# Loads of stored input differences two pairs ahead in the down projections of an encoder trunk

## The chip, the cores and the metric

The kernel runs on one core of one Trainium2 chip. The metric is the device time of one execution in microseconds (us). The core has a tensor engine (TensorE, PE in the profile; PEld is its weight load), a vector engine (DVE), a scalar engine (ACT), GpSimd (POOL) and a sync engine (SP) that only issues transfers; 16 DMA engines carry them. Each engine works through its own instructions in order.

## The reference

A trunk of two layers over 256 tokens of width 2048, in fp32. Each layer has one attention sub-layer and one MLP; the change touches the MLP only.

```
D_MODEL = 2048; SEQ = 256; DEPTH = 2; D_FF = 4 * D_MODEL
for i in range(DEPTH):
    h = rms_norm(x, norm_attn[i])
    ...
    # layer 0: differential attention, layer 1: windowed grouped-query attention with a sink,
    # both with 4 cross-attention heads into 256 memory tokens
    x = x + heads @ w_out[i]
    h = rms_norm(x, norm_mlp[i])
    x = x + jnp.square(jax.nn.relu(h @ w_up[i])) @ w_down[i]
```

## The kernel before

**Products.** Every fp32 operand is split into a rounded part hi (a cast on ACT, L439) and a remainder lo (a subtraction on DVE, L440), and every product is three matmuls: hi by hi, hi by lo, lo by hi (`three`, L531 to L533). A *piece* (`piece`, L417; `fetch`, L370) is a weight block of 128 x 1024 that SP loads (raw) and that is split so; a *pair* is two pieces, 256 rows of the weight. A pair is normally eight products (24 matmuls of 128 x 512). In the out, up and down projections some pairs take a seven-product scheme instead (`seven`, L548; 21 matmuls): it needs sums of weight blocks (made beforehand for layer 1 and part of layer 0 by two POOL transfers, a copy and an add in DRAM, L291 and L295, tiles *madesum*) and differences of the input blocks (`differences`, L538). In the down projection, the seven-product pairs are those of `FAST` (L50): 2, 4, 6, ..., 28 and 29 of 32.

**The MLP** (`mlp`, L984). The up projection ends in `to_hidden`: a block of hidden values is transposed, put through relu and square (ACT, L1020 and L1021), and for the blocks of `AWAY` stored to DRAM by POOL (L1024, *hid*), to be read back by SP later. A task some pairs later, `keep`, forms the differences of a seven-product pair j (128 x 2 x 512, hi and lo, 512 KB) in a tile of the tag "h2" and stores them to DRAM by POOL (L1000, *kept*). The down projection then runs twice over the 32 pairs, for the left and the right half of its 2048 columns. A pair of its loop asks for its first piece, for the split of the next pair's hidden block (`h2_of`, which also takes an "h2" tile; AHEAD is 2 pieces), for its second piece and, if it is a seven-product pair, loads its stored differences back into a further "h2" tile (L1118, `h<-kept`); then come its products. The stores of pairs 28 and 29 fall into the first pairs of the down projection.

**What sets the order.** The program is written in the order of these calls; the scheduler of the framework then places each engine's instructions by its own estimate of when they can run, so that an instruction can stand earlier or later in its engine's queue than in the code. The tag "h2" is a ring of six SBUF slots (`quad`, L91): a tile can only be written when all readers of the tile that held its slot before are done, a store to DRAM among them. Difference tiles to be stored, reloaded differences and hidden splits share this ring. The loads L1118 and the stores L1000 and L1024 stand in one queue on POOL, as do L291 and L295: a transfer that waits for its slot or its data holds up those behind it.

Of the kernel before, what the change touches and what calls it, by code (L numbers as in the profile page):

```python
# [22 lines left out]
P = 128  # L23
# [47 lines left out]
def trunk(ctx: ExitStack, tc: tile.TileContext, xin, xtok, memin, memtok, posrel, gcol, rows,  # L71
          w_a, w_b, w_mem, w_out, w_up, w_down, out):
    nc = tc.nc
# [188 lines left out]
    sums = {}  # L262
# [721 lines left out]
    def mlp(layer, X2, last):  # L984
        hT = []
        kept = {}
        wide = big([P, 6, 4, S])
        slots.clear()
        slots.extend(wide[:, i] for i in range(5))
        hidden_in.clear()  # L990

        def hidden(j):
            return hT[j // 2].rearrange("p k s -> p (k s)")[:, (j % 2) * 512:(j % 2) * 512 + 512]

        def keep(j):

            t2 = quad("h2", (P, 2, 512))
            differences(t2, hidden(j))
            kept[j] = dp.tile([P, 2, 512], F32R, name=nm("kept"))
            nc.gpsimd.dma_start(kept[j], t2)  # L1000

        name = f"up{layer}"
        diffs = {}

        def own_add(own, u):
            for n in range(2):
                for t in range(2):
                    nc.vector.tensor_tensor(u[n][t], own[n][t], u[n][t], op=ALU.add)

        def to_hidden(q, n, u, i, tag):  # L1010
            c = 2 * q + n
            if i == 0:
                hT.append(wide[:, 5] if c == 15 else blk([P, 4, S], F32))
            pt = bank(tag)
            for oo in range(2):
                for t in range(2):
                    o = 2 * i + oo
                    nc.tensor.transpose(out=pt[:, oo * S + t * P:oo * S + (t + 1) * P], in_=u[n][t][:, o * P:(o + 1) * P], identity=ident)  # L1018
            j = 2 * c + i
            nc.scalar.activation(hidden(j), pt, AF.Relu)  # L1020
            nc.scalar.activation(hidden(j), hidden(j), AF.Square)  # L1021
            if c in AWAY:
                hidden_in[j] = dp.tile([P, 512], F32, name=nm("hid"))
                nc.gpsimd.dma_start(hidden_in[j], hidden(j))  # L1024
            if any(j in fast_pairs(f"down{layer}", h) for h in range(2)):
                Task([Light(lambda: keep(j), 0)], wait=KEEP_AFTER[2 * n + i])

        for q in range(8):
            tag, other = ("mm", "aux") if q % 2 == 0 else ("aux", "mm")
            own = [[bank(tag) for _ in range(2)] for _ in range(2)]  # L1030
            fast = UP_FAST[q]
            for j in range(8):
                if j == fast[0]:
                    side = [bank(other) for _ in range(4)]
                if q == 0 and j in DIFF_UP:
                    i = DIFF_UP[j]
                    diffs[i] = quad("h2" if i == 2 else "blk", (P, 2, 512))
                    pair_differences(X2.pairs[i], diffs[i])
                two = [piece(name, q, 2 * j + i) for i in range(2)]
                pair = X2.pairs[j]  # L1040

                def at(kk, t, part):
                    return pair[:, kk, part, t * P:(t + 1) * P]

                if j in fast:
                    seven(own, side, j == fast[0], j == fast[-1], two, sums.pop((name, q, j)), at, diffs[j])
                elif j < 7:
                    for kk in range(2):
                        for t in range(2):
                            for n in range(2):  # L1050
                                one_of_eight(own, n, t, 2 * j + kk, KT - 1, two, at)
                else:
                    for n in range(2):
                        for t in range(2):
                            for kk in range(2):
                                one_of_eight(own, n, t, 2 * j + kk, KT - 1, two, at)
                if j == fast[-1]:
                    u = side_sums(side)
                for _ in range(2):
                    tick(2)  # L1060
            own_add(own, u)
            if q == 0:
                mlp_stats()
            Task([lambda q=q, u=u, n=n, i=i, tag=tag: to_hidden(q, n, u, i, tag) for n in range(2) for i in range(2)], wait=1, gap=0)
        slots.append(blk([P, 4, S], F32))
        N2 = Halves()
        while making:
            making.popleft()[1]()

        def h2_of(j):  # L1070
            t2 = quad("h2", (P, 2, 512))
            split(t2[:, 0, :], t2[:, 1, :], hids.pop(j) if j in hidden_in else hidden(j))
            return lambda kk, t, part: t2[:, part, kk * S + t * P:kk * S + (t + 1) * P]

        for half_ in range(2):
            tag = "mm" if half_ == 0 else "aux"
            ps = [[bank(tag) for _ in range(2)] for _ in range(2)]
            chunks = (2 * half_, 2 * half_ + 1)
            fast = fast_pairs(f"down{layer}", half_)
            plain_last = max(j for j in range(fast[-1]) if j not in fast)  # L1080

            def add_to(n, t, src, i=0):
                at = chunks[n] * 512 + i
                d = xt[:, t, at:at + src.shape[1]]
                nc.vector.scalar_tensor_tensor(d, src, r2[:, t:t + 1], d, op0=ALU.mult, op1=ALU.add)
                return at, d

            def finish(n, t, src, i=0):
                at, d = add_to(n, t, src, i)
                if last:  # L1090
                    nc.sync.dma_start(out[:, t * D + at:t * D + at + src.shape[1]], d)

            def by_columns(n, t):

                for i in (0, 256):
                    part_ = bank("mm")[:, 0:256]
                    for j, two, at in held:
                        for kk in range(2):
                            three(part_, j == held[0][0] and kk == 0, j == held[-1][0] and kk == 1,
                                  lambda part: at(kk, t, part), two[(kk + n) % 2], slice(n * 512 + i, n * 512 + i + 256))  # L1100
                    finish(n, t, part_, i)

            held = []
            ats = deque([h2_of(0)])
            for j in range(32):
                if j == fast[0]:
                    side = [bank("aux" if half_ == 0 else "mm") for _ in range(4)]
                two = [piece(f"down{layer}", half_, 2 * j)]
                if j < 31:
                    ats.append(h2_of(j + 1))  # L1110
                two.append(piece(f"down{layer}", half_, 2 * j + 1))
                at = ats.popleft()
                if last and half_ == 1 and j >= 30:
                    held.append((j, two, at))
                    continue
                if j in fast:
                    t2 = quad("h2", (P, 2, 512))
                    nc.gpsimd.dma_start(t2, kept[j])  # L1118
                    seven(ps, side, j == fast[0], j == fast[-1], two, sums.pop((f"down{layer}", half_, j)), at, t2)
                else:  # L1120
                    for kk in range(2):
                        for t in range(2):
                            for n in range(2):
                                own_last = 2 * plain_last + 1 if last and half_ == 1 and n == t == 1 else 4 * KT - 1
                                one_of_eight(ps, n, t, 2 * j + kk, own_last, two, at)
                if j == fast[-1]:
                    shared(side, add_to)
                    if last and half_ == 1:
                        add_to(1, 1, ps[1][1])
                for _ in range(2):  # L1130
                    tick(2)
            for n in range(2):
                for t in range(2):
                    if held and n == t == 1:
                        by_columns(n, t)
                        continue
                    for j, two, at in held:
                        for kk in range(2):
                            one_of_eight(ps, n, t, 2 * j + kk, 4 * KT - 1, two, at)
                    finish(n, t, ps[n][t])  # L1140
                if not last:
                    chunk_sq(chunks[n])
                    to_features(chunks[n], N2, G_ATTN + KT, tag)
        slots.clear()
        return N2
# [153 lines left out]
```

## Time and profile before

| | |
|---|---|
| time, median of 3 runs | 2088.14 us (2087.17, 2088.18, 2088.14) |
| the profiled execution's own time | 2087.19 us |
| its span | 2085.4 us |
| granted tensor clock, mean | 0.998 of full speed |
| busy: PE, DVE, ACT, POOL | 2073.3, 1771.0, 1275.6, 182.8 us |
| DMA, mean rate | 270 GB/s, 563.63 MB |
| loads of differences (L1118) | 59, of 512 KB each, median 5.8 us from issue to landing |

The down projection of layer 0 runs from about 770 us of the span on, that of layer 1 from about 1752 us to the end. A busy time says how long an engine had something to do; since the PE's matmuls overlap, a group's mean duration (some 390 ns) is longer than the distance from one start to the next. A wait is the idle time of an engine in front of an instruction, put down to the event that came last.

### The profile page before, as it was taken

To read this page: it belongs to the slowest core of one execution; us is meant where nothing else is said; L and a number is where in the kernel's file an instruction comes from. 1 tells how busy PE (TensorE), PEld (TensorE's weight loads), DVE (VectorE), ACT (ScalarE), POOL (GpSimd) and SP (SyncE) were. 2 spreads that over 40 slices of the span, in tenths; PEclk is the share of its full clock that TensorE was granted. 3 is DMA by queue.
4 is the path that set the end of the run, shared out by engine and by line. 5 is a ranking of instruction groups with operands and counts; after the bars stand their busy time and mean duration, and the time that the engine had idled before them with its cause. 6 is when DMAs were issued, how large, how long until landed. Compare 5 with 4: busy or idle time off the path is not lost.

```text
span 2085.4 us, 28771 instructions
## 1 busy us (share of the span) xinstructions
PE 2073.3 (99%) x10011; PEld 1721.3 (83%) x10011; DVE 1771.0 (85%) x2545; ACT 1275.6 (61%) x1892; POOL 182.8 (9%) x286
## 2 busy tenths in 40 slices
PE   9999999999999999999999999999999999999999
PEld 7878888888888878888888888888888887888887
DVE  7667778898999998899886677889999998889888
ACT  7457665566655666667655566566655666666664
POOL 1310100000011100000001100000001111000000
PEclk9999999999999999999999999999999999999999
DMA  9899864578899889988979975568889999998895
GB/s 315 300 295 280 264 206 157 189 255 245 266 288 300 257 289 314 338 279 294 330 267 287 266 233 198 170 210 242 252 273 300 285 282 346 306 332 305 295 332 170
DMA packets 168001, 563.63 MB, mean 270 GB/s; under 512 B 19456, under 2 KB 20480, under 8 KB 166656
## 3 DMA queue, kind: packets, MB, share of 16 engines
q1 hardware_dynamic: 132544, 439.62, 60.9%
q0 software_dynamic: 35168, 122.18, 21.9%
q8 instruction: 78, 1.28, 0.2%
q14 instruction: 67, 0.55, 0.1%
q10 hardware_dynamic: 144, 0.01, 0.0%
HBM read 531.19 MB, written 92.41 MB: 299 GB/s over the span
## 4 chain that ended last, share of the span: by engine, by line
PE 95%; DMA 2%; DVE 1%; issue 1%; ACT 1%; POOL 0%; SPq 0%; ACTq 0%; DVEq 0%; POOLq 0%
PE mm L531 12%; PE mm L532 12%; PE mm L533 12%; PE aux L532 11%; PE aux L533 11%; PE aux L531 11%; PE mm L492 7%; PE mm L493 7%; PE mm L494 7%; DMA h<-kept 1%; PE mm L1018 1%; PE aux L635 1%; DVE lo L440 1%; PE aux L612 1%; PE aux L654 1%
## 5 line engine op out<-in xcount | busy, mean ns | idle before, releaser
L439 ACT CAST hi<-raw 128x1024 fp32r<-128x1024 f32 (+1 forms) x522 | 525.4, 1036 | 451.1 <-issue 143.4
L440 DVE TENSOR_TENSOR lo<-raw,hi 128x1024 fp32r<-128x1024 f32 (+1 forms) x522 | 617.4, 1207 | 196.1 <-ACT hi L439 194.1
L492 PE MATMUL mm<-hi,x 128*128 128x512 f32 x640 | 256.0, 402 | 0.2 <-ACT hi L439 0.2
L493 PE MATMUL mm<-lo,x 128*128 128x512 f32 x640 | 251.0, 392 | 0.2 <-DVE lo L440 0.2
L494 PE MATMUL mm<-hi,x 128*128 128x512 f32 x640 | 250.3, 391 | 0.2 <-DVE x L436 0.2
L439 ACT CAST h<-big 128x1024 fp32r<-128x1024 f32 (+1 forms) x100 | 101.7, 1020 | 151.6 <-DVE big L283 129.6
L531 PE MATMUL mm<-hi,h 128*128 128x512 f32 (+1 forms) x461 | 179.8, 390 | 5.2 <-DMA h<-kept 5.0
L532 PE MATMUL mm<-lo,h 128*128 128x512 f32 (+1 forms) x461 | 179.1, 389 | 0.8 <-DVE lo L440 0.8
L533 PE MATMUL mm<-hi,h 128*128 128x512 f32 (+1 forms) x461 | 178.9, 388 | 0.0
L532 PE MATMUL aux<-lo,h 128*128 128x512 f32 x442 | 172.1, 389 | 0.1
L531 PE MATMUL aux<-hi,h 128*128 128x512 f32 x442 | 172.1, 390 | 0.0
L533 PE MATMUL aux<-hi,h 128*128 128x512 f32 x442 | 172.0, 389 | 0.0
L531 PE MATMUL mm<-hi,x 128*128 128x512 f32 x414 | 161.8, 391 | 0.0
L533 PE MATMUL mm<-hi,x 128*128 128x512 f32 x414 | 161.1, 389 | 0.0
L532 PE MATMUL mm<-lo,x 128*128 128x512 f32 x414 | 161.1, 389 | 0.0
L531 PE MATMUL aux<-hi,x 128*128 128x512 f32 x398 | 155.5, 391 | 0.0
L532 PE MATMUL aux<-lo,x 128*128 128x512 f32 x398 | 154.9, 389 | 0.0
L533 PE MATMUL aux<-hi,x 128*128 128x512 f32 x398 | 154.6, 389 | 0.0
L440 DVE TENSOR_TENSOR lo<-big,hi 128x1024 fp32r<-128x1024 f32 (+1 forms) x141 | 144.4, 1044 | 0.2 <-ACT hi L439 0.2
L494 PEld LDWEIGHTS mm<-hi,x 128*128 128x128 f32 x640 | 120.2, 188 | 26.1 <-DVE x L436 0.5
L492 PEld LDWEIGHTS mm<-hi,x 128*128 128x128 f32 x640 | 120.3, 188 | 24.7 <-ACT hi L439 1.0
L493 PEld LDWEIGHTS mm<-lo,x 128*128 128x128 f32 x640 | 120.5, 188 | 23.7 <-DVE lo L440 1.8
(309 smaller groups left out, 4193.7 us busy)
## 6 DMA issues: line engine op xcount, KB each, us to landing
raw<-in_w_up SPq DMA_DIRECT2D x164, 512.0 KB, 6.2
raw<-in_w_down SPq DMA_DIRECT2D x138, 512.0 KB, 5.7
madesum<-in_w_down POOLq DMA_DIRECT2D x118, 512.0 KB, 6.5
big<-in_w_up SPq DMA_DIRECT2D x92, 512.0 KB, 4.4
raw<-in_w_a SPq DMA_DIRECT2D x72, 512.0 KB, 5.5
h<-kept POOLq DMA_DIRECT2D x59, 512.0 KB, 5.8
raw<-in_w_out SPq DMA_DIRECT2D x52, 512.0 KB, 4.1
big<-madesum SPq DMA_DIRECT2D x49, 512.0 KB, 4.6
```

What stands on the lines that cost most here:

```text
L439: nc.scalar.copy(hi, src)
L440: return nc.vector.tensor_tensor(lo, src, as32(hi), op=ALU.subtract)
L492: nc.tensor.matmul(ps[t], lhsT=xh, rhs=hi[:, ws], start=(k == 0), stop=False)
L493: nc.tensor.matmul(ps[t], lhsT=xh, rhs=lo[:, ws], start=False, stop=False)
L494: nc.tensor.matmul(ps[t], lhsT=xl, rhs=hi[:, ws], start=False, stop=(k == KT - 1))
L531: nc.tensor.matmul(acc_, lhsT=x(0), rhs=w2[0][:, ws], start=first_, stop=False)
L532: nc.tensor.matmul(acc_, lhsT=x(0), rhs=w2[1][:, ws], start=False, stop=False)
L533: nc.tensor.matmul(acc_, lhsT=x(1), rhs=w2[0][:, ws], start=False, stop=last_)
L612: nc.tensor.transpose(out=pt[:, h * P:(h + 1) * P], in_=qn[t][:, h * P:(h + 1) * P], identity=ident)
L635: nc.tensor.transpose(out=pt[:, kt * S + qt * P:kt * S + (qt + 1) * P], in_=p_of(qt)[:, kt * P:(kt + 1) * P], identity=ident)
L654: nc.tensor.matmul(ps[c][:, qt * S:(qt + 1) * S], lhsT=qT[a][r, hl, qs], rhs=kT[b][r, hl, :], start=(a + b == 0), stop=(a == 1))
L1018: nc.tensor.transpose(out=pt[:, oo * S + t * P:oo * S + (t + 1) * P], in_=u[n][t][:, o * P:(o + 1) * P], identity=ident)
```

## The change

The load of a seven-product pair's differences is taken out of the pair's own place and put into a helper, `load_kept`, that takes the "h2" tile and issues the transfer. Pair j now calls it for pair j + 2, between its two pieces; a call ahead of the loop is for pair 1, which is not in `FAST` and so loads nothing. The first load of each half is that of pair 2, asked for by pair 0. Nothing is added to or taken from the computation.

```diff
             held = []
+            diff_in = {}
+
+            def load_kept(j):
+                if j in fast:
+                    diff_in[j] = quad("h2", (P, 2, 512))
+                    nc.gpsimd.dma_start(diff_in[j], kept[j])
+
+            load_kept(1)
             ats = deque([h2_of(0)])
             for j in range(32):
...
                 two = [piece(f"down{layer}", half_, 2 * j)]
                 if j < 31:
                     ats.append(h2_of(j + 1))
+                load_kept(j + 2)
                 two.append(piece(f"down{layer}", half_, 2 * j + 1))
...
                 if j in fast:
-                    t2 = quad("h2", (P, 2, 512))
-                    nc.gpsimd.dma_start(t2, kept[j])
-                    seven(ps, side, j == fast[0], j == fast[-1], two, sums.pop((f"down{layer}", half_, j)), at, t2)
+                    seven(ps, side, j == fast[0], j == fast[-1], two, sums.pop((f"down{layer}", half_, j)), at, diff_in.pop(j))
```

In the changed code the load is line 1109. The rows below are the engines' queues; the number behind a name is that of the tile, and it differs between the two kernels for the same tile.

**Layer 0, first pairs of the down projection, POOL.** L1000 stores differences (7629 those of pair 26, 7897 of pair 28, 7948 of pair 29), L1024 stores hidden blocks, L1118 loads the differences of pairs 2, 4 and 6 (kept_5310, 5565, 5692). Before:

```order
L1000 DMA kept_7629<-h_7622 128x1024
L1024 DMA hid_7816<-blk_7808 128x512
L1024 DMA hid_7825<-blk_7808 128x512
L1118 DMA h_7918<-kept_5310 128x1024
L1000 DMA kept_7897<-h_7890 128x1024
L1000 DMA kept_7948<-h_7941 128x1024
L1118 DMA h_8014<-kept_5565 128x1024
L1118 DMA h_8101<-kept_5692 128x1024
```

After:

```order
L1000 DMA kept_7629<-h_7622 128x1024
L1109 DMA h_7778<-kept_5310 128x1024
L1024 DMA hid_7818<-blk_7810 128x512
L1024 DMA hid_7827<-blk_7810 128x512
L1109 DMA h_7914<-kept_5565 128x1024
L1000 DMA kept_7899<-h_7892 128x1024
L1000 DMA kept_7950<-h_7943 128x1024
L1109 DMA h_8010<-kept_5692 128x1024
```

Each of the three loads has moved up: the first past two stores of hidden blocks, the second past the stores of pairs 28 and 29 into the place where the first load stood.

**The same place, PE.** These are products of pair 2; h_7859 (before) and h_7861 (after) are its hidden split, h_7918 and h_7778 its differences, and h_7909 is the hidden split of pair 3. Before:

```order
L531 MATMUL mm_7762<-hi_7862,h_7859 128x512
L532 MATMUL mm_7762<-lo_7863,h_7859 128x512
L533 MATMUL mm_7762<-hi_7862,h_7859 128x512
L531 MATMUL mm_7763<-x_7851,h_7859 128x512
L532 MATMUL mm_7763<-x_7852,h_7859 128x512
L533 MATMUL mm_7763<-x_7851,h_7859 128x512
L531 MATMUL mm_7762<-hi_7904,h_7909 128x512
L532 MATMUL mm_7762<-lo_7905,h_7909 128x512
L533 MATMUL mm_7762<-hi_7904,h_7909 128x512
L531 MATMUL mm_7764<-hi_7845,h_7918 128x512
```

After:

```order
L531 MATMUL mm_7762<-hi_7864,h_7861 128x512
L532 MATMUL mm_7762<-lo_7865,h_7861 128x512
L533 MATMUL mm_7762<-hi_7864,h_7861 128x512
L531 MATMUL mm_7764<-hi_7847,h_7778 128x512
L532 MATMUL mm_7764<-lo_7848,h_7778 128x512
L533 MATMUL mm_7764<-hi_7847,h_7778 128x512
L531 MATMUL aux_7902<-x_7851,h_7778 128x512
L532 MATMUL aux_7902<-x_7852,h_7778 128x512
L533 MATMUL aux_7902<-x_7851,h_7778 128x512
L531 MATMUL aux_7904<-x_7851,h_7778 128x512
```

Before, the seventh product of pair 2 and the first of pair 3 were placed ahead of the four that need the differences; now these four stand where the code has them. The same holds in layer 1; elsewhere PE's order is the same but for one product at the change of halves of layer 0.

**Layer 1, first pairs of the down projection, POOL.** L291 and L295 are the copies and adds of the weight sums; kept_14308, 14563 and 14690 are the differences of pairs 2, 4 and 6; the stores L1000 are those of pairs 28 and 29. Before:

```order
L291 DMA madesum_16737<-in_w_down 16x8192
L291 DMA madesum_16769<-in_w_down 16x8192
L295 DMA madesum_16737<-in_w_down 256x1x512
L295 DMA madesum_16769<-in_w_down 256x1x512
L1024 DMA hid_16826<-blk_16818 128x512
L1024 DMA hid_16835<-blk_16818 128x512
L1118 DMA h_16928<-kept_14308 128x1024
L1000 DMA kept_16907<-h_16900 128x1024
L1000 DMA kept_16958<-h_16951 128x1024
L1118 DMA h_17024<-kept_14563 128x1024
```

After:

```order
L291 DMA madesum_16737<-in_w_down 16x8192
L291 DMA madesum_16769<-in_w_down 16x8192
L1109 DMA h_16788<-kept_14308 128x1024
L295 DMA madesum_16737<-in_w_down 256x1x512
L295 DMA madesum_16769<-in_w_down 256x1x512
L1024 DMA hid_16828<-blk_16820 128x512
L1024 DMA hid_16837<-blk_16820 128x512
L1109 DMA h_16924<-kept_14563 128x1024
L1000 DMA kept_16909<-h_16902 128x1024
L1000 DMA kept_16960<-h_16953 128x1024
L1109 DMA h_17020<-kept_14690 128x1024
```

The first load now stands ahead of the two adds and two hidden stores, the second ahead of the stores of pairs 28 and 29.

**The same place, ACT, with the events that each cast waits for.** h_16978 and h_17015 (after: 16980 and 17017) are the hidden splits of pairs 4 and 5, h_17065 and h_17102 (17067 and 17104) those of pairs 6 and 7; hi_16981 (16983) belongs to pair 4's second piece, hi_17010 and hi_17019 (17012 and 17023) to pair 5. DMAHW stands for a landing of an SP transfer, DMASW for one of a POOL transfer; in the second list DMASW5 is the store of pair 28 and DMASW6 that of pair 29. Before:

```order
L439 CAST hi_16964<-big_13666 128x1024 [waits DMAHW6_49,DVE_49,PE_49]
L439 CAST h_16978<-blk_14481 128x512
L439 CAST hi_16981<-t2k_16853 128x512 [waits DMAHW5_49,PE_49]
L439 CAST h_17015<-blk_14481 128x512
L439 CAST h_17065<-blk_14496 128x512 [waits DMASW3_49,PE_49]
L439 CAST x_16970<-big_13666 128x1024 [waits DVE_49]
L439 CAST h_17102<-blk_14496 128x512 [waits DMASW5_49,Activation_49]
L439 CAST x_17055<-big_13666 128x1024 [waits DMAHW1_49]
L439 CAST hi_17010<-raw_17009 128x1024 [waits DMAHW6_49,PE_49]
```

After:

```order
L439 CAST hi_16966<-big_13666 128x1024 [waits DMAHW6_49,DVE_49,PE_49]
L439 CAST hi_16983<-t2k_16855 128x512 [waits DMAHW5_49,PE_49]
L439 CAST h_16980<-blk_14481 128x512 [waits DMASW5_49,DVE_49]
L439 CAST h_17017<-blk_14481 128x512 [waits DMASW7_49,PE_49]
L439 CAST x_16972<-big_13666 128x1024 [waits DVE_49]
L439 CAST h_17067<-blk_14496 128x512 [waits DMASW6_49,Activation_49]
L439 CAST x_17057<-big_13666 128x1024 [waits DMAHW1_49]
L439 CAST hi_17012<-raw_17011 128x1024 [waits DMAHW6_49,PE_49]
L439 CAST hi_17023<-raw_17022 128x1024 [waits DMAHW7_49,PE_49]
```

The hidden split of pair 4 (h_16980) waited for no transfer and now takes the slot of the differences of pair 28, so it waits for their store, with the cast of x behind it; that of pair 6 waits for the store of pair 29. In layer 0 the slots change hands in the same way.

## The prediction

> **What bounds the kernel now.** I read the page's busy times first, then what the tensor engine waited for, then a table by stages, and only then single instructions. In the rows of waits stand the us waited, how often, and the longest; in those of the stages (from:to, length) the busy us (and instructions) of PE, its weight loads, DVE, ACT and POOL, then the granted clock, the DMA engines' busy share and GB/s.
>
> ```profile
> PE 2073.3 (99%) x10011; PEld 1721.3 (83%) x10011; DVE 1771.0 (85%) x2545; ACT 1275.6 (61%) x1892; POOL 182.8 (9%) x286
> ...
> PE mm L531 <- DMA h<-kept: 5.0, 2, 2.6
> ...
> PE mm L532 <- DVE lo L440: 0.8, 1, 0.8
> ...
> 764.00:800.00 36.00, 33.38 (x154) 27.12 (x153) 30.59 (x41) 25.00 (x36) 3.78 (x8) 1.00 0.94 328
> 800.00:934.00 134.00, 134.00 (x593) 110.96 (x592) 119.78 (x139) 87.18 (x109) 6.87 (x13) 1.00 0.90 308
> ...
> 1750.00:1790.00 40.00, 36.67 (x157) 29.45 (x156) 31.17 (x42) 27.69 (x39) 4.37 (x8) 0.91 0.99 339
> ```
>
> PE is busy for 99% of the span, so nothing is won except where PE stands still or runs at a lower clock. Of 59 loads of differences (h<-kept, L1118) PE waited for two, 5.0 us in all. The table by stages says where: from 800 to 934 us PE has no idle time at all (134.00 of 134.00 us, 593 matmuls, so 0.226 us from one to the next), while the first 36 to 40 us of each layer's down projection lose 2.6 and 3.3 us, the second at a granted clock of 0.91. The ceiling of this change is therefore in two places: the first pairs of the down projection in layer 0 (from 770 us) and in layer 1 (from 1752 us). Everywhere else the other loads land in time already, and asking for them earlier can give nothing.
>
> **Layer 0, what goes.** PE's timeline, start and duration in us, in brackets the idle time before an instruction and what ended it:
>
> ```profile
> 775.66 0.39 PE L531 MATMUL aux<-hi,h 128*128 128x512 f32 x1
> ...
> 778.16 0.39 PE L533 MATMUL mm<-hi,h 128*128 128x512 f32 x1
> 781.03 0.51 PE L531 MATMUL mm<-hi,h 128*128 128x512 f32 x1 [2.48 <-DMA h<-kept]
> ...
> 790.35 0.50 PE L531 MATMUL mm<-hi,h 128*128 128x512 f32 x1
> ...
> 794.79 0.39 PE L532 MATMUL mm<-lo,h 128*128 128x512 f32 x1
> ```
>
> Pair 2, the first seven-product pair, starts at 775.66. From there to the second lo of pair 5 (794.79) are 21 + 24 + 21 + 4 = 70 matmuls, 15.8 us at 0.226; it took 19.13. So 3.3 us are lost, nearly all in front of the first load's product at 781.03, and 0.3 at the second's (790.35). Both loads stood late in POOL's queue:
>
> ```profile
> 771.76 1.08 POOL L1024 DMA_DIRECT2D hid<-blk  x2 [24.21 <-ACT blk L1021]
> 772.84 0.56 POOL L1118 DMA_DIRECT2D h<-kept  x1
> ...
> 755.76 0.39 PE L532 MATMUL mm<-h,blk 128*128 128x512 f32 x1
> ...
> 765.00:770.00 5.00, 5.00 (x31) 4.32 (x31) 5.00 (x7) 2.02 (x3) 0.00 (x0) 1.00 0.67 213
> ```
>
> The first load followed two stores of hidden blocks that waited 24 us for ACT. In the changed order it stands ahead of them and needs only its slot, whose last reader is the matmul at 755.76. It goes at about 756.3 and, even at the slowest landing seen (8.2 us, below), lands by 765, 12 us before pair 2 needs it. The DMA engines have room there (0.67 busy from 765 to 770). The second load takes the place of the first at 772.8 and lands by 781; pair 4 then starts at 785.9. Both waits go.
>
> **Layer 0, what is late next.** The loads now hold slots two pairs longer, so the ring of six "h2" slots hands out others. The hidden split of pair 4 gets the slot of the difference tile stored at 776.13 and that of pair 6 the one stored at 779.79, and both must wait for these stores to land; before, only one later split did.
>
> ```profile
> 786.89 0.62 ACT L439 CAST h<-blk 128x512 fp32r<-128x512 f32 x1 [1.19 <-DMA kept<-h]
> ...
> 789.45 2.36 DVE L440 TENSOR_TENSOR lo<-raw,hi 128x1024 fp32r<-128x1024 f32 x2
> ```
>
> That later split is visible: ACT goes on at 786.89, when the second store has landed. Behind it on ACT stand a cast of x and pair 5's two hi, and on DVE pair 5's two lo, ready at 789.45 + 2.36 = 791.81. PE, no longer held up, wants the second lo at 775.66 + 15.8 = 791.5. So the store takes over as the last wait, for 0.3 us, and the matmul of 794.79 comes at 791.9: **2.9 us saved** of 3.3. If the store lands 1 us later it is 1.9; if earlier, 3.3.
>
> **Layer 1, what goes.**
>
> ```profile
> 1757.88 0.39 PE L531 MATMUL aux<-hi,h 128*128 128x512 f32 x1
> ...
> 1761.28 0.50 PE L532 MATMUL mm<-lo,h 128*128 128x512 f32 x1 [0.76 <-DVE lo L440]
> ...
> 1764.58 0.79 PE L531 MATMUL mm<-hi,h 128*128 128x512 f32 x1 [2.57 <-DMA h<-kept]
> ...
> 1769.44 0.63 PE L533 MATMUL aux<-x,h 128*128 128x512 f32 x1
> ...
> 1775.66 0.39 PE L532 MATMUL mm<-lo,h 128*128 128x512 f32 x1
> ...
> 1765.00:1770.00 5.00, 5.00 (x13) 3.84 (x13) 2.04 (x3) 1.14 (x2) 0.53 (x1) 0.50 1.07 403
> ```
>
> From pair 2's start to the second lo of pair 4 (1775.66) are 21 + 24 + 4 = 49 matmuls, 11.1 us; it took 17.78. The 6.7 us are the wait for a lo of pair 3 that had been pulled ahead of the load's products (0.8), the wait for the load itself (2.6), and a halved clock: the granted clock is 0.50 from 1765 to 1770 and twelve matmuls (1764.58 to 1769.44 and its successor) run at 0.43 instead of 0.226 us, another 2.5. The changed PE order puts the load's products first again, so that lo has time.
>
> [...]
>
> **Layer 1, what is late next.** POOL, ACT and DVE, and the DMA share:
>
> ```profile
> 1737.70 1.02 POOL L291 DMA_DIRECT2D madesum<-in_w_down  x2 [7.93 <-DVE lo L440]
> ...
> 1759.60 0.54 POOL L1000 DMA_DIRECT2D kept<-h  x1 [2.65 <-DVE h L440]
> ...
> 1767.57 0.53 POOL L1118 DMA_DIRECT2D h<-kept  x1 [3.78 <-DMA kept<-h]
> ...
> 1766.79 0.61 ACT L439 CAST h<-blk 128x512 fp32r<-128x512 f32 x1
> ...
> 1770.63 1.04 ACT L439 CAST x<-big 128x1024 fp32r<-128x1024 f32 x1
> ...
> 1771.71 1.23 DVE L440 TENSOR_TENSOR x<-big,x 128x1024 fp32r<-128x1024 f32 x1 [4.67 <-ACT x L439]
> 1772.85 0.68 DVE L440 TENSOR_TENSOR lo<-t2k,hi 128x512 fp32r<-128x512 f32 x1
> ...
> 1740.00:1745.00 5.00, 5.00 (x23) 4.13 (x22) 5.00 (x9) 0.51 (x2) 1.09 (x1) 1.00 0.95 389
> ```
>
> The load now follows the two copies of 1737.70, at about 1738.8, long enough ahead. But the hidden split of pair 4 must now wait for the store issued at 1759.60. When that landed shows in POOL's row at 1767.57: about 1767.3. Behind this cast on ACT stand another h cast and the cast of x, behind that on DVE x and the second lo of pair 4: 1767.3 + 0.61 + 0.61 + 1.04 + 1.23 + 0.68 = 1771.5, against 1775.66 now. So at an unchanged landing **4.2 us** are saved of 6.7, and PE waits about 2.5 us in two parts instead.
>
> The landing won't stay unchanged. 512 KB that were asked for at 1756 now enter at 1738.8, and the second load stands where the first stood, ahead of the store. At 389 GB/s 0.52 MB are 1.35 us; the DMA engines were 0.95 busy then (and over 1.0 afterwards), which leaves a few tenths free. I take **1.0 us later**; the ends are 0, if the room suffices, and 2.8, if the load's own queue gets half of that rate. 4.2 - 1.0 = **3.2 us** in layer 1.
>
> POOL's queue already holds two copies there. [...]
>
> **What costs nothing.** No instruction is added: 59 loads before and after. Loads moved ahead of the stores of hidden blocks and of the madesum adds delay data that is read again only late in the down projection. In the steady stretch the hidden splits turn on four slots instead of six, and every second one stands behind two hi casts (about 2 us on ACT); the first row below says that they waited for PE, not PE for them, and PE had no idle time there. At the half change of layer 0 DVE makes a lo two operations earlier, PE wants it three matmuls earlier: 0 (ends -0.2 and +0.7).
>
> ```profile
> ACT h L439 <- PE aux L533: 32.3, 28, 2.7
> ...
> h<-kept POOLq DMA_DIRECT2D x59, 512.0 KB, 5.8
> ...
> L1118 POOL DMA_DIRECT2D h<-kept x59: 527/527/558, 772.8 to 2056.3; - x59
> ...
> DMA to landing us min/median/max: 3.7/5.8/8.2
> ```
>
> **Sum.** 2.9 + 3.2 = 6.1 us off the profiled execution's 2087.19 us (span 2085.4): 2081.1. The median of the runs shown is 2088.14, 0.95 above that execution; off the median it is 2082.0.
>
> **Rivals.**
> 1. *All stalls go* (the stores land 2 to 3 us sooner, as loads do at their fastest, 3.7 us): 3.3 + 6.7 = 10.0, so 2078.1. Against it: the DMA engines are full around both stores. Chance 0.13.
> 2. *The full queue takes layer 1's gain back*: the store lands 2.8 us later, and the t2k load that DVE waits for ahead of pair 2 comes 1.4 later too and puts the store itself off; nothing is left of 4.2, and 2.9 remain: 2085.2. For it: shares of 0.95 and more. Chance 0.17; a third of it stays above 4.2 us.
> 3. *The clock drops again*: the two waits that remain in layer 1 are within some 4 us, like the two that went ahead of 0.50. 6.1 - 2.5 = 3.6: 2084.5. For it the likeness, against it that they are shorter and layer 0's single wait cost no clock. Chance 0.10.
> 4. *It doesn't ask earlier*: POOL works its queue in order, and a load that is blocked by its slot would wait as before. 2088.1. The slots' last readers (755.76 in layer 0) speak against it. Chance 0.03.
> 5. *Slower*: in the steady stretch the hidden splits, now with four slots, reach PE too late. Each of the 57 remaining seven-product pairs would have to lose 0.18 us (10.3 us, the 6.1 gained and 4.2 more) before the kernel is slower by 0.2%; at 0.25 us each it is 2090. It decides once the splits slip by more than the three pairs (about 15 us) between slot and use; PE's 134.00 of 134.00 us speak against it. Chance 0.07.
>
> **The numbers.** Forecast 0.50, with a range of its own of 2080 to 2084. A measurement here can tell about 0.2% (4.2 us) from no change. Faster: 0.50 + 0.13 + 0.05 of rival 2 = 0.68. Within 0.2%: the rest of rival 2, rivals 3 and 4 = 0.25. Slower: 0.07. The range runs from rival 1 (2078.1) to rival 2 (2085.2), with about the 1.0 us on the slow side by which the runs shown differ: 2078 to 2086.5.
>
> **What would show it.** PE's waits for h<-kept vanish; ACT's "h <- DMA kept<-h" grows to several us around 783, 787, 1768 and 1771; the first loads go at about 756 and 1739; the clock is 1.00 from 1765 to 1770; the second lo of pair 5 in layer 0 comes at 791.9, that of pair 4 in layer 1 at 1775.66 - 3.2 - 2.9 = 1769.6. I am wrong if PE waits for the stores for more than 3 us in a layer, or loses time between 800 and 934.

## The result, and the profile after

| | before | after |
|---|---|---|
| median | 2087.65 us (10 runs) | 2083.26 us (10 runs) |
| lowest and highest | 2084.64 to 2089.64 | 2081.78 to 2085.18 |
| profiled execution, its span | 2087.19, 2085.4 | 2082.35, 2080.6 |

The ratio is 0.9981, 95% interval [0.9972, 0.9990]: 4.4 us off the median (2.1 to 5.8 by the interval's ends: 2087.65 times 0.0010 and 0.0028), where 6.1 were forecast: the time lies within the range that was given, while the interval of the saving ends short of 6.1. From the changed kernel's page, its list of what PE waited for, and its table by stages (columns as in the prediction):

```profile
PE 2071.5 (100%) x10011; PEld 1720.7 (83%) x10011; DVE 1769.7 (85%) x2545; ACT 1266.7 (61%) x1892; POOL 182.1 (9%) x286
```

```profile
PE mm L531 <- ACT hi L439: 1.4, 1, 1.4
PE mm L532 <- DVE lo L440: 1.3, 3, 0.6
```

```profile
764.00:800.00 36.00, 35.52 (x165) 29.31 (x164) 31.87 (x42) 26.58 (x38) 3.75 (x7) 1.00 0.95 335
800.00:934.00 134.00, 134.00 (x593) 111.00 (x592) 119.45 (x141) 84.26 (x109) 6.88 (x13) 1.00 0.90 309
...
1750.00:1790.00 40.00, 37.78 (x157) 30.16 (x157) 34.78 (x45) 28.14 (x39) 4.37 (x8) 0.96 1.01 360
1755.00:1760.00 5.00, 3.37 (x12) 2.18 (x12) 3.78 (x10) 5.00 (x9) 2.00 (x4) 0.91 1.03 397
1760.00:1765.00 5.00, 5.00 (x18) 3.98 (x17) 5.00 (x7) 3.35 (x5) 1.06 (x2) 0.75 1.09 397
```

The 5.0 us of waits for h<-kept are gone. Layer 0's first pairs now stand still for 0.5 us instead of 2.6. Layer 1's still lose 2.2 us of 40 and run at 0.96 of the clock: a wait for a hi on ACT has come in the place of the load.

Layer 0, PE, POOL, ACT and DVE of the changed kernel in order of time (start, duration, in brackets the idle time before and what ended it):

```profile
756.05 0.53 POOL L1109 DMA_DIRECT2D h<-kept  x1 [8.90 <-PE mm L533]
772.49 0.54 POOL L1109 DMA_DIRECT2D h<-kept  x1
775.26 0.39 PE L531 MATMUL aux<-hi,h 128*128 128x512 f32 x1
783.00 1.14 ACT L439 CAST h<-blk 128x512 fp32r<-128x512 f32 x2 [3.03 <-DMA kept<-h]
784.05 1.05 ACT L439 CAST x<-big 128x1024 fp32r<-128x1024 f32 x1
785.13 1.23 DVE L440 TENSOR_TENSOR x<-big,x 128x1024 fp32r<-128x1024 f32 x1 [0.78 <-ACT x L439]
786.27 0.68 DVE L440 TENSOR_TENSOR lo<-t2k,hi 128x512 fp32r<-128x512 f32 x1
787.01 0.50 PE L532 MATMUL mm<-lo,h 128*128 128x512 f32 x1 [0.48 <-DVE lo L440]
791.95 0.39 PE L532 MATMUL mm<-lo,h 128*128 128x512 f32 x1
```

Both loads go out when the prediction said. The one wait left is at pair 4's second lo: ACT stood still until the store of pair 28's differences had landed at 783.0, and two h casts, the cast of x, x on DVE and the lo followed.

Layer 1, the same:

```profile
1736.11 0.58 POOL L1109 DMA_DIRECT2D h<-kept  x1
1751.17 0.69 DVE L358 TENSOR_TENSOR big<-big,t2k 128x512 f32<-128x512 f32 x1 [2.35 <-DMA t2k<-in_w_down]
1755.29 0.39 PE L531 MATMUL aux<-hi,h 128*128 128x512 f32 x1
1756.85 0.63 ACT L439 CAST hi<-t2k 128x512 fp32r<-128x512 f32 x1
1757.54 0.50 PE L531 MATMUL mm<-hi,h 128*128 128x512 f32 x1 [1.40 <-ACT hi L439]
1759.51 0.63 PE L533 MATMUL mm<-hi,h 128*128 128x512 f32 x1
1767.00 1.14 ACT L439 CAST h<-blk 128x512 fp32r<-128x512 f32 x2 [3.65 <-DMA kept<-h]
1771.01 0.50 PE L532 MATMUL mm<-lo,h 128*128 128x512 f32 x1 [0.59 <-DVE lo L440]
```

Here DVE waits 2.35 us for a half piece that belongs to pair 2 (t2k<-in_w_down, which I call *t2k* below), ACT's relu and square and its hi of pair 2 come late behind it, PE stands still for 1.40, and the clock halves (0.50 from 1760 to 1762; matmuls of 0.63 us instead of 0.39 from 1759). How long t2k took, and its sister for pair 4, shows in the view of its line L341, cut to these two issues, with who waited for it (us, times): before, then after.

```profile
L341 SPq DMA_DIRECT2D t2k<-in_w_down x2: 328/400/472, 1741.2 to 1743.3; - x2
...
  DVE big L358: 1.5, 1
...
DMA to landing us min/median/max: 9.9/10.0/10.0
```

```profile
L341 SPq DMA_DIRECT2D t2k<-in_w_down x2: 328/381/434, 1738.6 to 1740.7; - x2
...
  DVE big L358: 2.4, 1
...
DMA to landing us min/median/max: 12.4/12.5/12.6
```

The first of the two was issued 2.6 us earlier, as PE came earlier from layer 0, but took 2.4 us longer and so landed almost where it had landed before (1741.2 + 10.0 and 1738.6 + 12.4). DVE had waited for it before already, for 1.5 us; it had nothing to spare.

### The profile page after: what moved, and what is told of

Its sections match the earlier page's. It is cut to its first block, busy times and chain, and to the rows that moved or that the text cites. A ratio compares the mean times of both kernels' runs of the same rounds, so it can differ in the third digit from the quotient of the medians.

```text
span 2080.6 us, 28646 instructions
## 1 busy us (share of the span) xinstructions
PE 2071.5 (100%) x10011; PEld 1720.7 (83%) x10011; DVE 1769.7 (85%) x2545; ACT 1266.7 (61%) x1892; POOL 182.1 (9%) x286
```

## The experiments

I took as the measure the stretch from pair 2's first product to the second lo of pair 4 (49 matmuls, 11.1 us without a loss) and on to that of pair 5 (70, 15.9), read from PE's timeline of each kernel's profile, and the landing time of t2k (median of the two).

| kernel | layer 0 | layer 1 | t2k | median, us | ratio to before, interval |
|---|---|---|---|---|---|
| before | 13.93 / 19.13 | 17.79 / 22.55 | 10.0 | | |
| before again (e8) | 14.83 / 19.67 | 14.52 / 20.95 | 8.8 | | |
| changed | 11.75 / 16.69 | 15.72 / 20.61 | 12.5 | 2083.26 | 0.9981 [0.9972, 0.9990] |
| changed again (e11) | 11.93 / 16.82 | 16.55 / 21.45 | 13.1 | | |
| layer 0 only (e1) | 12.69 / 17.59 | 16.35 / 21.11 | 10.2 | 2083.61 | 0.9980 [0.9972, 0.9989] |
| layer 1 only (e2) | 15.81 / 20.57 | 16.33 / 21.22 | 12.6 | 2086.48 | 0.9998 [0.9989, 1.0007] |
| sums earlier (e3) | 11.74 / 16.64 | 12.00 / 16.93 | 7.0 | 2079.41 | 0.9963 [0.9951, 0.9976] |
| stores in own slots (e4) | 11.11 / 15.87 | 13.10 / 17.91 | 12.1 | 2078.21 | 0.9959 [0.9946, 0.9973] |
| both (e5) | 11.11 / 15.87 | 11.11 / 15.87 | 7.8 | 2077.62 | 0.9958 [0.9945, 0.9970] |
| both, with the pair (e6) | 11.11 / 15.87 | 11.11 / 16.67 | 6.9 | 2077.53 | 0.9956 [0.9943, 0.9970] |
| first two early (e7) | 12.60 / 17.50 | 17.79 / 22.69 | 13.8 | 2084.80 | 0.9988 [0.9979, 0.9996] |
| own slots, with the pair (e9) | 11.11 / 16.25 | 13.41 / 19.71 | 12.2 | 2081.40 | 0.9974 [0.9963, 0.9984] |
| sums earlier, with the pair (e10) | 14.55 / 19.49 | 17.45 / 22.21 | 4.6 | 2086.34 | 0.9997 [0.9988, 1.0005] |

A column of two numbers gives the stretch to pair 4 and that to pair 5. The kernel before ran beside each group, at medians of 2086.90 to 2087.34 (2087.65 beside the change). All of these kernels lie within 0.5% of it, so a ratio counts as a difference only where its interval leaves out 1.

**e1 and e2, one layer each.** The distance is a parameter here (0 is the old place); the diff is that of e1, and in e2 its condition is `layer == 1`. The lines cut at the first mark make the calls ahead of the loop.

```diff
-            load_kept(1)
+            far = 2 if layer == 0 else 0
...
-                load_kept(j + 2)
+                if far:
+                    load_kept(j + far)
...
                 if j in fast:
+                    if not far:
+                        load_kept(j)
```

> Layer 0 asks two pairs ahead, layer 1 with the pair as before. Theory A (in layer 1 the early load itself takes DMA room from the weight loads of pairs 2 to 4): without it layer 1's load tk for pair 2 (first part L341) lands within about 10 us of its issue as before (9.99), PE waits for h<-kept again, and the stretch from pair 2 to the second lo of pair 4 takes 17.8 us as before; the kernel is about 2.4 us faster than before, all in layer 0 (stretch 16.7 instead of 19.1). Theory B (layer 1's losses come from PE arriving 2.6 us earlier at a place that the DMA engines pace): tk takes about 12.4 us although nothing is asked for early there, layer 1's stretch is about 2 us longer than before (19.8 to 20.2), and the gain over the whole kernel is below 1 us.

> Layer 1 asks two pairs ahead, layer 0 with the pair as before. Theory A: tk for pair 2 takes about 12.4 us from issue to landing as in the changed kernel, PE waits about 1.4 us for a hi at pair 2, the stretch from pair 2 to the second lo of pair 4 takes 15.7 us; about 2.1 us faster than before. Theory B: tk lands within about 10 us, PE doesn't wait at pair 2, the stretch takes 14.0 to 14.6 us; 3.2 to 4 us faster.

Theory A held in both on what sets t2k's time. With the load in its old place t2k took 10.2 us although PE came early from layer 0; with the early load 12.6 although PE came late. Theory B falls. Layer 0 alone is as fast as the whole change (2083.61 and 2083.26). Layer 1 alone can't be told from no change, where theory A expected 2.1 us, and in e1 the old layer 1 code took 16.35 us, not 17.8. For both misses e8 gives a reason. Layer 0 of e1, whose code is that of the changed kernel, took 17.59 us where 16.7 were expected: ACT went on behind the store's landing at 784.20 instead of 783.00, and PE waited 1.43 us for pair 4's second lo instead of 0.48. So this wait, too, differs from one execution to another.

**e8 and e11, the same two kernels again.**

> The kernel before once more, for a second profile of the two stretches. The same layer 0 code has now taken 13.93 us (before) and 15.81 us (e2) from pair 2 to the second lo of pair 4, and the same layer 1 code 17.79 (before) and 16.35 (e1). If these are scatter of one execution against another (the clock halves behind a wait or it doesn't), both values or others between 13.5 and 18 come again, with a granted clock below 1 where the stretch is long; if they are effects of the other layer's code, this profile repeats 13.9 and 17.8 within 0.3 us.

> The changed kernel once more, for a second profile. If the first was typical, layer 0's stretch to pair 5's second lo takes 16.6 to 17.6 us (16.69, and 17.59 in e1), layer 1's 20.6 to 21.2 (20.61, and 21.22 in e2), tk for pair 2 again takes 12 to 13 us to land and PE waits 1 to 2 us for a hi at pair 2. If the first was an outlier, layer 1's stretch is below 19.5.

PE's waits of before again, and the row of its table by stages that had a clock of 0.50 in the first profile:

```profile
PE mm L531 <- DMA h<-kept: 7.8, 3, 3.4
```

```profile
1765.00:1770.00 5.00, 5.00 (x24) 4.13 (x23) 2.38 (x4) 3.19 (x5) 0.54 (x1) 1.00 1.06 410
```

The first profile of before was one draw. Layer 1 took 22.55 us there with a halved clock, 20.95 in e8, where waits of 3.38 us (layer 0) and 3.07 (layer 1) cost no clock at all (1.00 from 764 to 800 and from 1750 to 1790), and 21.11 in e1, with a clock of 0.76 from 1760 to 1765. Not all of the scatter is the clock's: e8's layer 0 took longer than before's at a clock of 1.00, since the load landed later (a wait of 3.38 instead of 2.48), and its layer 1 holds a third wait of 1.37, for the load of pair 4. With the change: 20.61, 21.22 and 21.45. e11 repeats the first profile of the changed kernel to within 0.9 us; its layer 1 and t2k lie a little above what was expected. So the layer 1 part is worth 21.54 - 21.09 = 0.4 us by these means. Layer 0 without the change took 19.13, 19.67, 20.57 and 19.49, with it 16.69, 16.82, 17.59 and 16.64: 19.72 - 16.94 = 2.8 us. Each mean is of three or four profiles that differ by 0.8 to 1.6 us among themselves. The two stretches together give 3.2 us of the 4.4 by the medians; what is left lies within the interval of these (2.1 to 5.8) and I have not located it.

**e3, fewer transfers beside t2k.** In layer 1 the weight sums are made every 7 pieces, so that the last two copies and adds are over before the down projection:

```diff
-            at += SUM_GAP if at < quiet else SUM_GAP_UP
+            at += SUM_GAP if at < quiet else (7 if layer == 1 else SUM_GAP_UP)
```

> As the changed kernel, but in layer 1 the weight sums are copied and added every 7 pieces of the up projection instead of every 8, so that the last two copies and two adds (512 KB each) are done before the down projection begins. Theory A (the DMA engines are full between 1735 and 1755 us and tk's lateness is their sharing): tk for pair 2 lands in 8 to 9 us instead of 12.4, PE's wait for hi at pair 2 (1.40) and the halved clock behind it go, the store of pair 28 is issued and lands about 2 us earlier, and the stretch to the second lo of pair 4 takes 12 to 13.5 us instead of 15.7; 2 to 3.7 us faster than the changed kernel. Rival (tk is late for another reason, its own issue or its queue's order): the stretch stays at 15 to 16 us and the kernel within 0.7 us of the changed one. The earlier sums could cost a little in the up projection, where the share of the DMA engines is 0.84 to 1.03.

```profile
L341 SPq DMA_DIRECT2D t2k<-in_w_down x2: 328/380/433, 1739.2 to 1741.3; - x2
...
DMA to landing us min/median/max: 6.3/7.0/7.7
```

```profile
1755.00:1760.00 5.00, 5.00 (x24) 4.14 (x23) 4.91 (x7) 5.00 (x8) 0.54 (x1) 1.00 0.96 351
1760.00:1765.00 5.00, 5.00 (x24) 4.14 (x23) 3.67 (x5) 1.74 (x5) 1.07 (x2) 1.00 1.09 403
```

t2k lands in 7.0 us, PE stands still nowhere from 1755 to 1765 at a clock of 1.00, and the stretch to pair 4 takes 12.0. Its lateness in the changed kernel came from the transfers beside it. The table shows both kinds of them: t2k took 12.1 to 13.8 us with the early load and the sums (six profiles), 8.8 to 10.2 with the sums alone (three), 6.9 to 7.8 with the early load alone (e3, e5, e6) and 4.6 with neither (e10). In the 5 us in which it was under way in both kernels the DMA engines were about as full in one as in the other, first the changed kernel, then e3:

```profile
1740.00:1745.00 5.00, 5.00 (x24) 4.14 (x23) 4.75 (x8) 1.28 (x2) 2.17 (x2) 1.00 0.98 367
1740.00:1745.00 5.00, 5.00 (x24) 4.14 (x23) 5.00 (x9) 2.11 (x2) 0.00 (x0) 1.00 1.03 398
```

So what counted was which transfers were under way beside t2k; in what order the engines serve them, no run shows. What is left in e3 is the store: 0.47 and 0.73 us in front of pair 4's second lo.

**e4, the stores' slots.**

```diff
-            t2 = quad("h2", (P, 2, 512))
+            t2 = quad("x2" if j >= 28 else "h2", (P, 2, 512))
```

> As the changed kernel, but the differences of pairs 28 and 29 are put into slots of the tag x2, which are free then, instead of h2; no hidden split takes a slot that one of these stores has to clear. Theory S (behind the load the stores' landing is the last wait): ACT's waits for kept<-h go, the waits of 0.48 us (layer 0) and 0.59 us (layer 1) in front of pair 4's second lo go; layer 0's stretch takes 15.8 to 16.0 instead of 16.7, layer 1's about 14.6 to 15.1 (the wait for tk and the halved clock stay); 1.2 to 1.8 us faster than the changed kernel. Rival (the lo is late for DVE's or ACT's own queue, or the next load is): within 0.4 us of it.

Layer 0 now runs without a loss, 15.87:

```profile
764.00:800.00 36.00, 36.00 (x168) 30.04 (x167) 33.07 (x43) 26.11 (x37) 3.77 (x7) 1.00 0.98 348
```

Theory S holds for the two waits, but the edit is worth 5.0 us by the medians and 0.8 + 2.7 by the two stretches, not 1.2 to 1.8; the rest of the 5.0 I have not located. The edit also does more than it was meant to: the second load, of pair 4, now goes ahead of the hidden stores, at 1742.41 instead of 1755.89 in layer 1 and at 756.76 instead of 772.49 in layer 0. So it is not the stores' slots alone that e4 changes.

```profile
756.76 0.54 POOL L1109 DMA_DIRECT2D h<-kept  x1 [1.05 <-PE aux L533]
```

In layer 1 t2k was as late as before (12.1) and PE waited 1.2 us for the same hi, but the clock stayed at 1.00: of the 2.7 us, 0.59 are the store's and about 1.6 the eight matmuls that took 0.43 instead of 0.226 us from one to the next in the changed kernel's profile.

**e5, both.**

> Both edits of e3 and e4 on the changed kernel: in layer 1 the sums every 7 pieces, and the differences of pairs 28 and 29 in slots of the tag x2. If the two remaining waits are what e3 and e4 took them for (the sharing of the DMA engines behind tk, the stores behind the hidden splits), each edit takes the part the other left: layer 0's stretch from pair 2 to the second lo of pair 4 takes 11.1 us as in e4, layer 1's 11.1 to 11.5 us (12.0 in e3, 13.1 in e4), PE waits for nothing in either place, and the kernel takes 2076 to 2077.5 us. Rival (a third wait is hidden behind these two, a late load of differences or a late lo): layer 1 keeps 12 us or more and the time stays at e4's 2078.

```profile
1750.00:1790.00 40.00, 40.00 (x181) 33.22 (x180) 35.76 (x46) 30.55 (x43) 3.76 (x7) 1.00 0.92 333
```

Both places run without a loss: no third wait stood behind the two. The kernel gains only 0.6 us on e4, and one reason is the stretch between the two places: from pair 7 in layer 0 to pair 2 in layer 1 it took 955.84 us against 954.19 in e4. It took 955.21 in e3 and 954.89 in e6, but 953.82 in e10, and 953.39 to 954.31 in all kernels with the sums every 8 pieces. The earlier sums seem to take back there a part of what they give.

**e6, both edits without the early load.**

> The two edits of e5 on the kernel before, which asks for the differences with the pair. Theory: the two edits remove waits that stand behind the late first load and can't remove the load's own. PE still waits for h<-kept at pair 2 in both layers (2 to 3 us each), layer 0's stretch to the second lo of pair 4 takes 13 to 14 us; 4 to 6 us slower than e5, 2081 to 2084. Rival (the early load isn't needed once the other transfers are out of its way): no wait for h<-kept over 0.5 us in layer 1, and within 2 us of e5.

```profile
756.77 0.54 POOL L1118 DMA_DIRECT2D h<-kept  x1 [10.25 <-PE aux L533]
770.73 1.08 POOL L1024 DMA_DIRECT2D hid<-blk  x2 [13.42 <-ACT blk L1021]
```

```profile
PE mm L531 <- DMA h<-kept: 0.5, 1, 0.5
```

My theory fell, and this is the run that says most. The code asks with the pair, and yet the first load is issued at 756.77, ahead of the hidden stores. In the kernel before, too, its slot was free at about that time, since its last reader ran at 757.35, but it stood behind these stores in POOL's queue and went at 772.84:

```profile
757.35 0.39 PE L533 MATMUL aux<-h,x 128*128 128x512 f32 x1
```

With two tiles fewer in the ring the scheduler placed it ahead of them. How the scheduler comes to that I have not traced. The kernel is as fast as e5 (2077.53 and 2077.62).

**e9 and e10, each edit alone on the kernel before.**

> The kernel before with one edit: the differences of pairs 28 and 29 in slots of the tag x2; the loads stay with the pair, the sums every 8 pieces. Theory P (what held the first load back in the kernel before was its slot in the ring, not its place in the code: in e6 it was issued at 756.8 and 1736.8 us though asked for with the pair): the first loads go at about 757 and 1738, PE's waits for h<-kept fall from about 5 to at most 1 us, layer 0's stretch to pair 5's second lo takes 15.9 us, layer 1's 17 to 19 as in e4 (17.9), since the sums still share the DMA engines with it; 2078 to 2080, as fast as e4 (2078.2) within 1.5 us. Rival (the code's place decides, and e6 owed its time to the moved sums): PE waits for h<-kept for 4 us or more and the time is over 2081.

> The kernel before with one edit: in layer 1 the sums every 7 pieces. Theory: the first load of layer 1 still stands behind the two hidden stores in POOL's queue, so PE still waits for it, but on emptier DMA engines it lands sooner; layer 1's stretch to pair 5's second lo takes 17.5 to 19.5 us instead of 21 to 22.5, layer 0's stays at 19 to 20.6; 2 to 4 us faster than before, 2083 to 2085.5. Rival (the sums were all that held layer 1 up): layer 1's stretch takes under 16.7 us, 2082 or less.

e9, POOL, and what PE waited for:

```profile
757.18 0.53 POOL L1118 DMA_DIRECT2D h<-kept  x1 [10.26 <-PE aux L533]
```

```profile
PE mm L531 <- ACT hi L439: 1.5, 1, 1.5
PE mm L531 <- DMA h<-kept: 1.2, 1, 1.2
```

What theory P forecast for the first loads came: they went at 757.18 and 1736.20 with the code's place unchanged. Its reason did not hold: it was not the slot that had held the load back, free at 757.35 in the kernel before too, but the place in the queue. Layer 1 took 19.71, not 17 to 19, PE waited 1.2 us, not at most 1, and the time is 2081.4, not 2078 to 2080: the second load, of pair 4, now comes last. Beside this edit the early request is worth 2081.40 - 2078.21 = 3.2 us by medians of two groups of runs, whose intervals overlap. e10 was a miss:

```profile
PE mm L531 <- DMA h<-kept: 6.5, 2, 3.4
```

t2k landed in 4.6 us, and nothing was won, since the load behind the hidden stores was still the last to come. The edits don't add up: the early request alone gives 4.4 us, the sums alone 0.6 (not to be told from 0), the two together 2087.32 - 2079.41 = 7.9.

**e7, only the first two loads of a half early.**

```diff
-                load_kept(j + 2)
+                if j in (0, 2):
+                    load_kept(j + 2)
...
                 if j in fast:
+                    if j > 4:
+                        load_kept(j)
```

> Only the loads of pairs 2 and 4 of each half are asked for two pairs ahead, the other 51 with the pair as before. Theory (nothing is won away from the first pairs): the same time as the changed kernel, within 0.8 us; PE has no idle time from 800 to 934 us. Rival (the early requests help the steady stretch too, or its four slots cost something there): slower or faster by over 1 us, with idle time of PE between 800 and 934 or after 1790 us.

```profile
800.00:934.00 134.00, 134.00 (x592) 110.94 (x592) 118.59 (x139) 86.41 (x109) 6.91 (x13) 1.00 0.92 313
```

```profile
783.14 1.67 ACT L439 CAST h<-blk 128x512 fp32r<-128x512 f32 x3 [3.35 <-DMA kept<-h]
787.67 0.50 PE L532 MATMUL mm<-lo,h 128*128 128x512 f32 x1 [1.33 <-DVE lo L440]
```

It is 1.5 us slower than the changed kernel, not within 0.8, though the two intervals overlap, and PE has no idle time from 800 to 934: what difference there is lies in the first pairs again. In layer 0 three hidden casts instead of two now stand between the store's landing and the cast of x, and the wait for pair 4's second lo is 1.33 instead of 0.48; since it was 1.43 in e1 with two casts, the third cast (0.53 us) is not shown to be the cause. In layer 1, t2k took 13.8 us and PE waited 2.73 us for pair 2's hi, which accounts for the larger part: 22.69 us instead of 20.61.

## Why the prediction came out right, and what it had wrong in layer 1

The time of 2083.26 lies in the range of 2078 to 2086.5, and in the forecast's own of 2080 to 2084. The path was right: the two loads no longer stop PE, and the stores' landings are waits behind them; in layer 1 one more wait came, t2k's, that the sum left out. That the time came out within 1.3 us of 2082.0 is in part luck: the saving was 4.4 us and not 6.1, and the kernel before ran at 2087.65 here, 0.5 us below the 2088.14 that the forecast started from.

1. **Layer 0: right.** The loads were to go at about 756.3 and 772.8 and went at 756.05 and 772.49; 2.9 us were to be saved, and the profiles' means give 2.8 (the first pair of them 19.13 - 16.69 = 2.4). The closeness of 2.8 is in part luck, too: the mean without the change holds a longer wait (3.38 in e8) and a lowered clock (0.89 from 775 to 790 in e2), and the wait left with it was larger than the 0.3 us of the sum.
2. **What is late next in layer 0: a store's landing, as forecast, but the other store.** I followed the store of pair 29 to pair 5's lo (0.3 us), and did not follow that of pair 28 to pair 4's as I did in layer 1. The same sum gives 783.0 + 0.61 + 0.61 + 1.04 + 1.23 + 0.68 = 787.2 there; PE went on at 787.01, and pair 5's lo came without a wait.
3. **Layer 1: the term of 1.0 us failed.** The prediction let the early load delay only the store of pair 28, by 1.0 us. It delayed t2k, by about 3 us (12.5, 13.1 and 12.6 with it, 10.0, 8.8 and 10.2 without), and so everything behind it: pair 2's hi and the differences that are stored. Counted from pair 2's start, the store landed after 1766.9 - 1755.3 = 11.6 us, against 1767.3 - 1757.9 = 9.4 before: 2.2 us later, not 1.0. That was rival 2's mechanism, with 1.4 for t2k where about 3 came; as far as three profiles on each side can tell, the 0.4 us that their means leave in layer 1 are nearer to that rival's nothing than to the forecast's 3.2, and the whole saving of 4.4 lies between its 2.9 and the forecast's 6.1. PE went on at pair 4's second lo at 1771.01, not at 1769.6.
4. **Layer 1's 6.7 us weren't all the load's.** 2.5 of them were a halved clock, which I took for a fixed part of the loss. It came in some profiles (before 0.50; changed 0.75 from 1760 to 1765) and not in others (e8), so a part of it was the draw of that execution. Forecast were 3.2; the profiles' means give 0.4, and e2's times can't be told from those of the kernel before.
5. **Rival 3** happened too in this sense: the clock dropped again, to 0.75 behind a wait of 1.40 and one of 0.23 us, and to 0.81 in e11 behind one of 2.01; in e2 it stayed at 1.00 behind one of 1.89.
6. **The rest: right.** From 800 to 934 PE is busy for 134.00 of 134.00 us as before, and from pair 7 of layer 0 to pair 2 of layer 1 it took 954.05 us against 953.80. So rival 5 did not come; its second figure is a slip: 57 pairs at 0.25 us each are 14.3 us, 2082.0 + 14.3 = 2096 and not 2090. In the same way half of 389 GB/s makes the end of the term 2.7, not 2.8; neither changes the forecast.
7. **Rival 4, that it doesn't ask earlier**, is wrong for this change; but e6 and e9 show that its question was the right one: with the line in the code unchanged, another place in POOL's queue moved the first load from 772.84 to 756.77 and 757.18.

## What to carry to other kernels

Before a transfer is asked for earlier, list what else lands in the window that it moves into, and ask which of those landings has no slack: in layer 1 the half piece that DVE already waited for (1.5 us) paid for this load (12.5 us to landing instead of 10.0), not only the store that I watched. A request's line in the code is worth little where a ring of slots and an in-order queue decide when it goes (here 772.84 in the kernel before and 756.77 in e6 from one line): look at its place in the queue, and at who shares its ring. And where a stretch of the profile holds a lowered clock (here 0.50 in one profile of before and 1.00 in the other), profile the kernel a second time before that loss is put into a sum.

## What the runs showed that I had not expected

- Waits of nearly one length were followed by a lowered clock in one execution and not in another: 3.42 us in e10 by a granted clock of 0.61, 3.38 and 3.07 in e8 by 1.00; 1.40 in the changed kernel by 0.75, 1.46 in e9 by 1.00.

```profile
1765.00:1770.00 5.00, 5.00 (x15) 3.92 (x15) 0.00 (x0) 2.27 (x4) 0.54 (x1) 0.61 1.06 409
```

This row is from e10's table by stages. What decides between the two, no run here shows.
- Two edits that touch no load of differences, made on the kernel before, gave 2087.34 - 2077.53 = 9.8 us, over twice the change's 4.4, and with them in place the change is worth nothing that these runs can show (2077.62 in e5, 2077.53 in e6).
